# Layer 1's MLP by seven block products, its hidden layer through DRAM

## The chip, the core and the metric

One core of a Trainium2 chip runs the whole program. Its engines are TensorE (PE in the profile; PEld is its weight load), VectorE (DVE), ScalarE (ACT), GpSimd (POOL) and SyncE (SP, which issues the DMAs here). The metric is the device time of one execution in microseconds (us). All data is fp32.

## The reference

Two transformer layers over 1024 latent tokens and 256 context tokens, width 1024. Both layers have a mixer (attention) and a squared-ReLU MLP of width 4096, each between RMS norms with shift, scale and gate. After layer 1 only the latent tokens are kept, so its MLP works on 1024 tokens:

```python
def squared_relu_mlp(h, w1, w2):
    return jnp.square(jax.nn.relu(h @ w1)) @ w2

f_x = squared_relu_mlp(modulate(rms_norm(x, norm_g[l, 2]), sh2_x, sc2_x), w_mlp_in[l], w_mlp_out[l])
x = x + g2_x * rms_norm(f_x, norm_g[l, 3])
```

Here h is 1024 x 1024, w1 1024 x 4096 and w2 4096 x 1024: two matrix products of the same size.

## The kernel before, in words

The stages follow one another: layer 0 with its attention and its MLP, layer 1's input projection, its attention, its output projection and, from some 2551 us of the profiled execution, its MLP. The change is in the last two.

**A product.** Every fp32 operand of a projection or of the MLP is split into a high part (fp32r, the rounded form that TensorE takes) and a low part, the rest. `split` copies the high part on one engine and subtracts it from the source on another. `dense` adds three matmuls per 128 rows of the contraction: high by high, high by low, low by high. Each multiplies a stationary 128x128 block with a moving 128x512 one into a PSUM bank of 512 columns.

**Slots.** `R` hands out tiles of 128x1024 (4 KB a partition) by hand, with a life that says how long their memory stays. 12 of them live throughout; each span of the kernel adds its own. A slot is overwritten only once its last reader is done.

**The output projection** works tile by tile (128 tokens). A tile's two products go through `residual` (ACT squares, POOL's power, DVE's scaling, a sum on POOL or DVE) and then, one tile later, through `norm_T`: a norm, 8 transposes on TensorE, and `norm_half`, which applies scale and shift (ACT for the first half of the width, DVE for the second) and splits the result h into slots of `X` (`MlpIn`), in two chunks of 512 tokens.

**The MLP** (`mlp`) goes through 16 blocks of 256 hidden columns. A block's up products are two chunks of tokens by two 128-column halves, 24 matmuls each; ACT applies the ReLU, DVE squares and makes the high part, POOL the low part, and the result stays in slots. Its down products are 8 tiles by two halves of the width, 6 matmuls each; DVE adds each onto `acc`, a tile of 128x1024 per token tile, also in SBUF (the first block is copied by ACT). W1's and W2's blocks come through `stg`, a pool of two 128x1024 staging buffers, and are split by ACT and POOL during the block before. In the last block the tiles are finished in turn: a norm, the gate and the residual (`finish1`), then the store to the output. Inputs of the residual are loaded two tiles ahead, from three buffers.

**Order.** Tile's scheduler orders each engine's instructions from a timeline of its own; only where `manual_schedule` stands (attention, the last block of an MLP) is an engine's order as written. On the chip each engine's queue is worked off in that fixed order.

## Time and profile before

| what | value |
|---|---|
| median of three runs | 3286.07 us (3283.56 to 3288.95) |
| profiled execution | 3286.25 us, span 3284.4 us |
| TensorE busy | 3196.6 us, 97% of the span |
| DVE, ACT, POOL busy | 1547.1, 1117.9, 1056.1 us |
| mean granted clock of TensorE | 0.991 of full speed |
| layer 1's MLP | about 2551 to 3264 us of the span |

The span runs from the first to the last instruction; the execution's own time is 1.9 us longer. Busy time of TensorE counts each matmul from its start to its modelled end. Matmuls overlap, so how many of them fit into a stretch is read from their starts, not from their durations. A row of the timeline ends, in brackets, with the idle time before it and with what ended it.

### The profile page before, as it was taken

How to read it: one execution, taken by the hardware profiler on the slowest of the kernel's cores; microseconds unless marked ns; L12 is line 12 of the kernel's file. 1: busy time of each engine (PE TensorE's matmuls, PEld its weight loads, DVE VectorE, ACT ScalarE, POOL GpSimd, SP SyncE). 2: the span in 40 equal slices, each digit the busy share in tenths (PEclk: the TensorE clock that was granted, in tenths of full speed). 3: DMA queues.
4: the chain of work that ended last, by engine and by line, in shares of the span. 5: the costliest groups of instructions: out<-in, count | busy, mean ns of one | idle time of the engine just before them, and what ended most of it. 6: DMA issues, size and time to landing. Idle time of an engine off the chain costs nothing.

```text
span 3284.4 us, 47529 instructions
## 1 busy us (share of the span) xinstructions
PE 3196.6 (97%) x18421; PEld 2611.4 (80%) x18421; DVE 1547.1 (47%) x3295; ACT 1117.9 (34%) x2315; POOL 1056.1 (32%) x878
## 2 busy tenths in 40 slices
PE   8999999999999999999999989999989999999997
PEld 3777888887887777777778878998878788888886
DVE  3345476798462343343343561148755333333335
ACT  4212576788342111111111242257864311111111
POOL 2346100035452232232232453210334533333333
PEclk9999999999999999999999999999999999999999
DMA  7566312132432222222121146124454211111113
GB/s 242 166 150 177 81 53 57 55 85 87 138 116 84 71 63 84 64 71 85 57 65 39 58 145 153 44 60 118 130 152 127 73 45 52 52 45 51 46 46 96
DMA packets 221569, 294.00 MB, mean 90 GB/s; under 512 B 36800, under 2 KB 154064, under 8 KB 221344
## 3 DMA queue, kind: packets, MB, share of 16 engines
q1 hardware_dynamic: 221248, 290.71, 30.0%
q8 instruction: 145, 2.38, 0.3%
q14 instruction: 80, 0.66, 0.1%
q0 software_dynamic: 96, 0.26, 0.0%
HBM read 240.01 MB, written 50.89 MB: 89 GB/s over the span
## 4 chain that ended last, share of the span: by engine, by line
PE 75%; DVE 3%; issue 2%; DMA 2%; POOL 1%; ACT 1%; SPq 0%; POOLq 0%; ACTq 0%; DVEq 0%
PE mm L382 20%; PE mm L383 19%; PE mm L384 19%; PE po L1081 2%; PE tp L1060 2%; PE po L913 2%; PE md L246 1%; PE S L515 1%; PE X L516 1%; PE X L515 1%; PE S L516 1%; PE po L808 1%; PE tp L892 1%; PE tp L790 1%; POOL s L193 1%
## 5 line engine op out<-in xcount | busy, mean ns | idle before, releaser
L1198 DVE TENSOR_TENSOR acc<-mm,acc 128x512 f32<-128x512 f32 x540 | 369.1, 689 | 388.1 <-PE mm L384 387.1
L193 POOL TENSOR_TENSOR r<-ws,r 128x1024 fp32r<-128x1024 f32 x146 | 356.9, 2449 | 539.5 <-ACT r L186 534.8
L384 PE MATMUL mm<-s,r 128*128 128x512 f32 (+1 forms) x1404 | 516.6, 368 | 0.0
L383 PE MATMUL mm<-s,r 128*128 128x512 f32 (+1 forms) x1404 | 515.5, 367 | 0.0
L382 PE MATMUL mm<-s,r 128*128 128x512 f32 (+1 forms) x1404 | 513.5, 366 | 1.7 <-DVE s L188 1.7
L1184 DVE TENSOR_TENSOR hr<-hr 128x512 f32<-128x512 f32 (+1 forms) x160 | 134.4, 840 | 612.7 <-ACT hr L1183 612.6
L382 PE MATMUL mm<-r,r 128*128 128x512 f32 x1046 | 413.5, 395 | 0.3 <-DVE r L188 0.3
L383 PE MATMUL mm<-r,r 128*128 128x512 f32 x1046 | 408.5, 391 | 0.0
L384 PE MATMUL mm<-r,r 128*128 128x512 f32 x1046 | 407.9, 390 | 0.0
L186 ACT ACTIVATE r<-ws 128x1024 fp32r<-128x1024 f32 x155 | 164.4, 1061 | 709.2 <-PE mm L384 336.8
L193 POOL TENSOR_TENSOR r<-hr,r 128x512 fp32r<-128x512 f32 (+1 forms) x130 | 167.0, 1285 | 562.6 <-DVE r L188 559.2
L1183 ACT ACTIVATE hr<-mm 128x512 f32<-128x512 f32 (+1 forms) x160 | 88.3, 552 | 644.4 <-PE mm L384 638.4
L382 PEld LDWEIGHTS mm<-s,r 128*128 128x128 f32 x1404 | 264.2, 188 | 50.6 <-DVE s L188 1.9
L383 PEld LDWEIGHTS mm<-s,r 128*128 128x128 f32 x1404 | 264.7, 189 | 49.2
L384 PEld LDWEIGHTS mm<-s,r 128*128 128x128 f32 x1404 | 264.1, 188 | 46.1
L382 PEld LDWEIGHTS mm<-r,r 128*128 128x128 f32 x1046 | 196.2, 188 | 80.7 <-DVE acc L1198 36.9
L384 PEld LDWEIGHTS mm<-r,r 128*128 128x128 f32 x1046 | 196.3, 188 | 43.0 <-POOL r L193 0.9
L383 PEld LDWEIGHTS mm<-r,r 128*128 128x128 f32 x1046 | 196.4, 188 | 39.1
L713 ACT ACTIVATE P<-P,nm 128x1280 f32<-128x1280 f32 (+1 forms) x160 | 190.2, 1190 | 31.1 <-DVE P L721 28.7
L382 PE MATMUL mm<-r,e 128*128 128x512 f32 (+1 forms) x496 | 192.6, 389 | 1.3 <-ACT e L186 1.3
L383 PE MATMUL mm<-r,e 128*128 128x512 f32 (+1 forms) x496 | 190.9, 385 | 0.0
L384 PE MATMUL mm<-r,e 128*128 128x512 f32 (+1 forms) x496 | 189.8, 385 | 0.4 <-POOL e L193 0.4
(256 smaller groups left out, 6011.3 us busy)
## 6 DMA issues: line engine op xcount, KB each, us to landing
wm<-in_w_mod_dram SPq DMA_DIRECT2D x80, 512.0 KB
ws<-in_w_mlp_in_dram SPq DMA_DIRECT2D x64, 512.0 KB
ws<-in_w_mlp_out_dram SPq DMA_DIRECT2D x64, 512.0 KB
q<-qT SPq DMA_DIRECT2D x224, 128.0 KB
ws<-in_w_in_dram SPq DMA_DIRECT2D x36, 512.0 KB
xres<-xn SPq DMA_DIRECT2D x18, 512.0 KB
x<-xres SPq DMA_DIRECT2D x18, 512.0 KB
wm<-in_w_mod_dram SPq DMA_DIRECT2D x32, 256.0 KB
```

The source lines that it names most:

```text
L186: act.activation(o, i, AF.Copy)
L193: lo_eng.tensor_tensor(lo, src, f(hi), op=OP.subtract)
L382: pe.matmul(pt, sh, mh, start=k == 0, stop=False)
L383: pe.matmul(pt, sh, ml, start=False, stop=False)
L384: pe.matmul(pt, sl, mh, start=False, stop=k == n - 1)
L515: pe.matmul(dst, q[0], k, start=True, stop=False)
L516: pe.matmul(dst, q[1], k, start=False, stop=True)
L713: act.activation(P, P, AF.Exp, scale=-1.0, bias=self.nm[:, u:u + 1], accum_out=self.sums[:, u:u + 1])
L913: pe.matmul(self.po, VB[self.h][:, kt, :], self.pt[:, kt, :], start=kt == self.kts[0], stop=kt == self.kts[-1])
L1183: act.activation(r, pt, AF.Relu)
L1184: dve.tensor_tensor(r, r, r, op=OP.mult)
L1198: dve.tensor_tensor(acc[t][:, s], pt, acc[t][:, s], op=OP.add)
```

## The change

Both of the MLP's matrix products are cut into 2x2 blocks, and the four result blocks are formed from seven block products instead of eight (Strassen's method, in Winograd's form). `SEVEN` names, for either side, which operand block or which sum of blocks enters product 1 to 7; `TURN` is their order. Three PSUM banks take the products of a turn: 1, 6, 7 and 4 add up in bank b, product 2 is in a, 5 and 3 add up in c, and what b or c holds after each product is taken out before the next one adds to it.

**Up** (`up7`). The blocks of h are two halves of the width by two halves of the tokens (`Tokens7`: four raw tiles of 128x4x512). `norm_half` now writes h raw; only products 1 and 2, which take blocks 11 and 21 as they are, are split tile by tile. The other five operands come from `rest`, which forms its sums in place and splits them, called in front of the fifth product. W1 goes in 16 units of 256 columns. POOL forms the sums (4 of 7 products), ACT the high part and DVE the low part; a product's operand is one slot, and products are prepared six ahead. A product has 12 matmuls. ACT and DVE combine the results, and the squared ReLU goes to `hT`, a new tensor in DRAM, 4096 x 1024.

**Down** (`Down7`). The hidden layer comes back from `hT`, for 256 tokens and the rows of a unit. There are six units of 3, 3, 3, 3, 2 and 2 pairs of 128 hidden rows (m, with g as the index), four passes over pairs of token tiles in each (j), seven products in each pass; a product has 3m matmuls. The token side is stationary: DVE forms sums (4 of 7) and low parts, ACT the high parts, six products ahead. The weight side moves: for each g and product one slot, its sums and low part by POOL, its high part by ACT. Of the 28 slots, 21 hold unit 0 and 7 one g of unit 1. In the last pass of a unit, `weights` prepares m further operands after each product, in the slots that it freed. DVE adds each product's bank onto `acc` (in unit 0, ACT copies four of seven). After product 4 of a pass in the last unit, both of its tiles are finished.

The slots of h come free in the last up unit, product by product, and the down half's first operands go there. `bg`, a bias buffer of earlier stages, moves to a pool of its own, which is closed before layer 1's attention. The residual's input has one buffer now, and it is loaded when a tile is finished.

```diff
+UNITS1 = (3, 3, 3, 3, 2, 2)
...
+    def dense(pt, sta, mov, first=True, group=True):
+        n, free = len(sta), not group
         for k in range(n):
             (sh, sl), (mh, ml) = sta[k], mov[k]
-            pe.matmul(pt, sh, mh, start=k == 0, stop=False)
-            pe.matmul(pt, sh, ml, start=False, stop=False)
-            pe.matmul(pt, sl, mh, start=False, stop=k == n - 1)
+            pe.matmul(pt, sh, mh, start=first and k == 0, stop=False, skip_group_check=free)
+            pe.matmul(pt, sh, ml, start=False, stop=False, skip_group_check=free)
+            pe.matmul(pt, sl, mh, start=False, stop=k == n - 1, skip_group_check=free)
...
+    SEVEN = {"S": {1: (11,), 2: (12,), 4: (22,), 5: (21, OP.add, 22), 6: (5, OP.subtract, 11),
+                   7: (11, OP.subtract, 21), 3: (12, OP.subtract, 6)},
+             "T": {1: (11,), 2: (21,), 3: (22,), 5: (12, OP.subtract, 11), 6: (22, OP.subtract, 5),
+                   7: (22, OP.subtract, 12), 4: (21, OP.subtract, 6)}}
+    TURN = (1, 2, 6, 5, 7, 3, 4)
...
+        def get(self, p):
+            if p not in self.q:
+                r = self.rule[p]
+                if len(r) == 1:
+                    self.q[p] = self.q[r[0]]
+                else:
+                    a, b = self.get(r[0]), self.get(r[2])
+                    o = self.temp()
+                    self.add.tensor_tensor(o, a, b, op=r[1])
+                    self.q[p] = o
+            return self.q[p]
...
+        def rest(self, p, lo_eng=dve):
+            q = self.q
+            for c in range(2):
+                k = slice(2 * c, 2 * c + 2)
+                b11, b12, b21, b22 = (q[x][:, k, :] for x in (11, 12, 21, 22))
+                a, b = self.slots(p)[c]
+                if p == 5:
+                    dve.tensor_tensor(b11, b12, b11, op=OP.subtract)
+                elif p == 7:
+                    dve.tensor_tensor(b12, b22, b12, op=OP.subtract)
+                elif p == 6:
+                    dve.tensor_tensor(b22, b22, b11, op=OP.subtract)
+                elif p == 4:
+                    dve.tensor_tensor(b21, b21, b22, op=OP.subtract)
+                split(a, b, {5: b11, 7: b12, 3: b22, 6: b22, 4: b21}[p], act, lo_eng)
...
+            s = R.get(0)
+            v = s.view([128, 2, 4, 128])
+            split(v[:, 0], v[:, 1], W[u].get(p), act, dve)
+            ops[u, p] = s, [(v[:, 0, k, :], v[:, 1, k, :]) for k in range(4)]
...
+        for i, (u, p) in enumerate(seq):
+            if i < 14 and p not in (1, 2) and u == 0:
+                if p == 6:
+                    for x in (5, 7, 3, 6):
+                        X.rest(x)
+                elif p == 5:
+                    X.rest(4)
+            ready(len(seq) if u == n - 1 else i + ahead)
+            k = {1: "b", 2: "a", 5: "c"}.get(p)
+            if k:
+                st[u, k] = ps.tile([128, 512], F32, name=k, tag=k, bufs=2)
+            b = st[u, {1: "b", 6: "b", 7: "b", 4: "b", 2: "a", 5: "c", 3: "c"}[p]]
+            s, sta = ops.pop((u, p))
+            dense(b, sta, X.parts(p), first=k is not None, group=False)
+            s.free()
+            if u == n - 1:
+                X.free(p)
+                freed(p)
...
+            def put(fh, th, other):
+                t = tmp.tile([128, 512], F32, tag="ht", name="ht", bufs=2)
+                r = tmp.tile([128, 512], F32, tag="hr", name="hr", bufs=2)
+                if other is None:
+                    act.activation(t, b, AF.Relu)
+                    dve.tensor_tensor(r, t, t, op=OP.mult)
+                else:
+                    dve.tensor_tensor(t, b, other, op=OP.add)
+                    dve.scalar_tensor_tensor(r, t, 0.0, t, op0=OP.max, op1=OP.mult)
+                sp.dma_start(hT[u * 256 + fh * 128:u * 256 + (fh + 1) * 128, th * 512:(th + 1) * 512], r)
...
+        def weights(self, n, tmp):
+            for _ in range(min(n, len(self.todo))):
+                ui, g, p = self.todo.pop(0)
+                f0, m = self.units[ui]
+                if (ui, g) not in self.raw:
+                    r = []
+                    for x in (f0 + g, f0 + m + g):
+                        w = stg.tile([128, 1024], F32, tag="stg", name="ws", bufs=NSTG)
+                        sp.dma_start(w, w_mlp_out[self.l, x * 128:(x + 1) * 128, :])
+                        r.append(w)
+                    self.raw[ui, g] = Seven("T", {10 * (f + 1) + h + 1: r[f][:, h * 512:(h + 1) * 512]
+                                                  for f in range(2) for h in range(2)},
+                                            lambda: tmp().tile([128, 512], F32, tag="cm", name="cm", bufs=3), pool)
+                s = R.get(1)
+                v = s.view([128, 2, 512])
+                split(v[:, 0], v[:, 1], self.raw[ui, g].get(p), act, pool)
+                self.W[ui, g, p] = s, (v[:, 0], v[:, 1])
...
+                if (ui, j) not in H:
+                    raw = tmp.tile([128, 2 * mx, 256], F32, tag="hw", name="hw", bufs=2)[:, :2 * m]
+                    sp.dma_start(raw, self.hT[f0 * 128:(f0 + 2 * m) * 128, j * 256:(j + 1) * 256]
+                                 .rearrange("(a p) t -> p a t", p=128))
+                    H[ui, j] = Seven("S", {10 * (t + 1) + fh + 1: raw[:, fh * m:(fh + 1) * m, t * 128:(t + 1) * 128]
+                                           for t in range(2) for fh in range(2)},
+                                     lambda: tmp.tile([128, mx, 128], F32, tag="ch", name="ch", bufs=3)[:, :m], dve)
+                v = tmp.tile([128, 2, mx, 128], F32R, tag="ho", name="ho", bufs=ahead + 1)
+                split(v[:, 0, :m], v[:, 1, :m], H[ui, j].get(p), act, dve)
+                ops[ui, j, p] = [(v[:, 0, k, :], v[:, 1, k, :]) for k in range(m)]
...
+                k = {1: "b", 2: "a", 5: "c"}.get(p)
+                if k:
+                    st[k] = ps.tile([128, 512], F32, name=k, tag=k, bufs=2)
+                b = st[{1: "b", 6: "b", 7: "b", 4: "b", 2: "a", 5: "c", 3: "c"}[p]]
+                dense(b, ops.pop((ui, j, p)), [self.W[ui, g, p][1] for g in range(m)], first=k is not None, group=False)
+                if j == self.npairs - 1:
+                    for g in range(m):
+                        self.W.pop((ui, g, p))[0].free()
+                    self.weights(m, lambda: tmp)
+                t, h = {1: (0, 0), 2: (0, 0), 6: (0, 1), 3: (0, 1), 7: (1, 1), 5: (1, 1), 4: (1, 0)}[p]
+                o = acc[2 * j + t][:, h * 512:(h + 1) * 512]
+                if ui == 0 and p in (1, 6, 5, 4):
+                    act.activation(o, b, AF.Copy)
+                else:
+                    dve.tensor_tensor(o, b, o, op=OP.add)
+                if last and p == 4:
+                    for x in (2 * j, 2 * j + 1):
+                        finish(x, acc[x])
...
-    span = ExitStack()
-    R.add(span.enter_context(tc.tile_pool(name="span1", bufs=1, reuse_waits="tile")), 20, "s1", 1)
-    mid = span.enter_context(tc.tile_pool(name="mid1", bufs=1, reuse_waits="tile"))
-    ps = span.enter_context(tc.tile_pool(name="ps4", bufs=1, space=PSUM, reuse_waits="tile"))
-    X3 = MlpIn(T)
+    span, xs, sup = ExitStack(), ExitStack(), ExitStack()
+    R.add(span.enter_context(tc.tile_pool(name="span1", bufs=1, reuse_waits="tile")), 16, "s1", 1)
+    wp = ExitStack()
+    R.add(wp.enter_context(tc.tile_pool(name="wp0", bufs=1, reuse_waits="tile")), 4, "w0")
+    ps = sup.enter_context(tc.tile_pool(name="ps4", bufs=1, space=PSUM, reuse_waits="tile"))
+    X3 = Tokens7(xs.enter_context(tc.tile_pool(name="xraw", bufs=1, side="right", reuse_waits="tile")))
...
+    D1 = Down7(1, UNITS1, 4, hT, None)
+    ph = ExitStack()
+    R.add(ph.enter_context(tc.tile_pool(name="wp1", bufs=1, reuse_waits="tile")), 3, "w1")
+    tmp = ph.enter_context(tc.tile_pool(name="t5", bufs=1, reuse_waits="tile"))
+    ps = ph.enter_context(tc.tile_pool(name="ps5", bufs=1, space=PSUM, reuse_waits="tile"))
+    n7 = [0]
+    def freed(p):
+        n7[0] += 1
+        D1.weights((4, 4, 4, 4, 4, 1, 0)[n7[0] - 1], lambda: tmp)
+    for _ in up7(1, X3, ps, tmp, hT, 6, 4, freed):
+        pass
+    ph.close()
+    R.drop(7)
+    wp.close()
+    xs.close()
...
     def finish1(j, acc):
-        if j + XA < 8:
-            load1(j + XA)
-        residual([acc], G2[0], xts[j], acc, ps, pool if FIN1[j % len(FIN1)] == "P" else dve)
+        xt = tmp.tile([128, 1024], F32, tag="x", name="x", bufs=1)
+        sp.dma_start(xt, xres[2][j * 128:(j + 1) * 128, :])
+        residual([acc], G2[0], xt, acc, ps, pool if FIN1[j % len(FIN1)] == "P" else dve)
         sp.dma_start(block(out[0], j), acc)
 
-    with tc.tile_pool(name="t5", bufs=1, reuse_waits="tile") as tmp:
-        mlp(1, X3, 8, ps, mid, tmp, W1, finish1, last1,
-            [("up", 0), ("up", 1, 0), ("down", 0), ("down", 1), ("up", 1, 1), ("free", 0), ("free", 1), ("w1", 0)]
-            + [("down", i) for i in range(2, 8)])
+    D1.weights(7, lambda: tmp)
+    D1.run(acc, ps, tmp, 6, finish1, last1)
+    ph.close()
```

## Rows read from the trace of the kernel before

**Rows 1.** The page: busy us of each engine, share of the span, instructions.

```profile
PE 3196.6 (97%) x18421; PEld 2611.4 (80%) x18421; DVE 1547.1 (47%) x3295; ACT 1117.9 (34%) x2315; POOL 1056.1 (32%) x878
```

**Rows 2.** Busy time by stretch: stretch, us, engines (instructions), TensorE clock, DMA share, GB/s.

```profile
2563.00:2568.00 5.00, 1.78 (x12) 1.22 (x11) 3.80 (x11) 2.10 (x5) 2.64 (x4) 1.00 0.00 0
...
2700.00:3200.00 500.00, 500.00 (x2172) 407.48 (x2171) 183.05 (x269) 75.57 (x93) 167.95 (x92) 1.00 0.15 47
...
3200.00:3265.00 65.00, 64.17 (x280) 52.18 (x278) 36.54 (x52) 14.11 (x33) 26.90 (x18) 1.00 0.25 70
```

**Rows 3.** Timeline of TensorE: start, us; 15 starts in a row, then 51.

```profile
2699.70 0.39 PE L382 MATMUL mm<-s,r 128*128 128x512 f32 x1
...
2702.96 0.40 PE L384 MATMUL mm<-s,r 128*128 128x512 f32 x1
...
3252.45 0.39 PE L382 MATMUL mm<-r,r 128*128 128x512 f32 x1
...
3263.78 0.39 PE L384 MATMUL mm<-r,r 128*128 128x512 f32 x1
```

**Rows 4.** Groups of instructions, 2551 us on: count | busy us, mean ns | idle before.

```profile
L382 PE MATMUL mm<-s,r 128*128 128x512 f32 x512 | 201.1, 393 | 1.7 <-DVE s L188 1.7
...
L1198 DVE TENSOR_TENSOR acc<-mm,acc 128x512 f32<-128x512 f32 x240 | 165.3, 689 | 187.1 <-PE mm L384 186.5
...
L193 POOL TENSOR_TENSOR r<-hr,r 128x512 fp32r<-128x512 f32 x64 | 82.4, 1287 | 232.4 <-DVE r L188 232.0 <-DVE n1m L180 0.4
...
L1128 POOL TENSOR_TENSOR acc<-acc,x 128x1024 f32<-128x1024 f32 x6 | 15.7, 2612 | 8.0 <-DVE acc L1127 4.6 <-DVE nrm L180 1.9 <-ACT hr L1183 1.5
```

**Rows 5.** The same groups over the whole span: DVE by shape.

```profile
L193 DVE TENSOR_TENSOR s<-ws,s 128x1024 fp32r<-128x1024 f32 x4 | 5.0, 1290 | 12.0 <-ACT s L186 12.0
...
L1690 DVE TENSOR_TENSOR q<-tp,q 128x256 fp32r<-128x256 f32 x32 | 13.4, 418 | 2.4 <-ACT q L186 2.3
```

**Rows 6.** Timeline of DVE and of POOL at three places.

```profile
2713.79 1.91 DVE L1184 TENSOR_TENSOR hr<-hr 128x512 f32<-128x512 f32 x1
...
2712.75 2.40 POOL L193 TENSOR_TENSOR r<-ws,r 128x1024 fp32r<-128x1024 f32 x1 [0.40 <-ACT r L186]
...
2724.08 0.69 DVE L1198 TENSOR_TENSOR acc<-mm,acc 128x512 f32<-128x512 f32 x1 [0.67 <-PE mm L384]
...
2723.23 2.40 POOL L193 TENSOR_TENSOR r<-ws,r 128x1024 fp32r<-128x1024 f32 x1 [5.22 <-ACT r L186]
...
3247.21 1.28 DVE L1127 SCALAR_TENSOR_TENSOR acc<-acc,nrr,gate 128x1024 f32<-128x1024 f32 x1 [2.96 <-POOL nrr L181]
...
3248.54 0.69 DVE L1184 TENSOR_TENSOR hr<-hr 128x512 f32<-128x512 f32 x1
...
3248.64 2.85 POOL L1128 TENSOR_TENSOR acc<-acc,x 128x1024 f32<-128x1024 f32 x1 [1.46 <-ACT hr L1183]
```

**Rows 7.** Timeline at the start of the MLP: TensorE, ACT, DVE.

```profile
2564.84 1.09 PE L308 MATMUL tr<-ident,xt 128*128 128x128 f32 x8 [1.56 <-DVE xt L301]
...
2567.60 0.73 PE L382 MATMUL mm<-s,r 128*128 128x512 f32 x2 [1.66 <-DVE s L188]
...
2552.97 1.06 ACT L186 ACTIVATE r<-ws 128x1024 fp32r<-128x1024 f32 x1 [1.62 <-DMA ws<-in_w_mlp_out_dram]
...
2553.94 0.58 ACT L178 ACTIVATE xn<-mm 128x512 f32<-128x512 f32 x1
...
2558.82 1.22 DVE L1128 TENSOR_TENSOR xn<-xn,xt 128x1024 f32<-128x1024 f32 x1
...
2565.98 1.37 DVE L315 TENSOR_SCALAR h<-tr,mcols 128x128 f32<-128x128 f32 x4
```

**Rows 8.** Chain of waits (start, us, what); SP's waits, 2500:2600 (total, times, longest).

```profile
2549.43 3.52 DMA ws<-in_w_mlp_out_dram
...
SPq L353 <- POOL r L193: 37.1, 5, 23.1
```

**Rows 9.** Chain of waits at the end of the span.

```profile
3266.56 9.05 DMA x<-xres
```

More of the change, by code (lines that the diff above doesn't have):

```diff
@@ L394, in hybrid_dit_kernel @@
     os0 = dscr([NT * 128, 1024], "os0")
+    hT = dscr([FF, T], "hT")
     def block(a, j):
@@ L1296, in out_projection, with __init__ @@
         return out
+    SEVEN = {"S": {1: (11,), 2: (12,), 4: (22,), 5: (21, OP.add, 22), 6: (5, OP.subtract, 11),
[3 more added lines that the diff above has]
+    TURN = (1, 2, 6, 5, 7, 3, 4)
+    class Seven:
+        def __init__(self, side, blocks, temp, add):
+            self.rule, self.q, self.temp, self.add = SEVEN[side], dict(blocks), temp, add
+        def get(self, p):
[9 more added lines that the diff above has]
+            return self.q[p]
@@ new lines, in hybrid_dit_kernel, with __init__, slots, tile @@
+    class Tokens7:
+        def __init__(self, pool):
+            self.q = {10 * (kh + 1) + th + 1: pool.tile([128, 4, 512], F32, name=f"xq{kh}{th}")
+                      for kh in range(2) for th in range(2)}
+            self.s = {}
+        def slots(self, p):
+            if p not in self.s:
+                self.s[p] = [(R.get(1), R.get(1)) for _ in range(2)]
+            return [tuple(x.view([128, 2, 512]) for x in ab) for ab in self.s[p]]
+        def tile(self, i):
+            th, o = divmod(i, 4)
+            o = slice(o * 128, (o + 1) * 128)
+            def parts(h):
+                if th:
+                    return []
+                return [(2 * c, 2, a[:, :, o], b[:, :, o]) for c, (a, b) in enumerate(self.slots(1 + h))]
+            parts.raw = lambda h: self.q[10 * (h + 1) + th + 1][:, :, o]
+            return parts
+        def rest(self, p, lo_eng=dve):
[13 more added lines that the diff above has]
+                split(a, b, {5: b11, 7: b12, 3: b22, 6: b22, 4: b21}[p], act, lo_eng)
+        def parts(self, p):
+            return [(a[:, k, :], b[:, k, :]) for a, b in self.slots(p) for k in range(2)]
+        def free(self, p):
+            for ab in self.s.pop(p):
+                for x in ab:
+                    x.free()
@@ L1754, in last1 @@
+    ph.close()
+    R.drop(7)
+    wp.close()
+    xs.close()
+    ph = ExitStack()
+    tmp = ph.enter_context(tc.tile_pool(name="t6", bufs=1, reuse_waits="tile"))
+    ps = ph.enter_context(tc.tile_pool(name="ps6", bufs=1, space=PSUM, reuse_waits="tile"))
+    acc = [tmp.tile([128, 1024], F32, name=f"acc{t}") for t in range(8)]
+    G2 = {}
     def last1():
-        gate_next(1, 0)
-        for j in range(XA):
-            load1(j)
+        G2[0] = stg.tile([128, 1024], F32, tag="stg", name="gate", bufs=NSTG)
+        mod_vec(G2[0], 1, 5, 0)
```

97 lines of the change are left out of this document (81 added, 16 removed).

## The prediction

> **What bounds the kernel now.** I read the page's busy shares first, then a table by stretches of layer 1's MLP, then matmul starts in the timeline, then the other engines beside them. TensorE is busy 97% of the span [rows 1], and in the MLP (2551 to 3264 us) its only gap is near 2565, of 3.2 us in two waits; in 2700 to 3200 us DVE is busy 183 of 500 us, ACT 76, POOL 168 [rows 2]. So this stretch is bound by the number of matmuls and by nothing else. A matmul's 390 ns is latency: starts lie (2702.96 - 2699.70)/14 = 0.2329 us apart in an up product and (3263.78 - 3252.45)/50 = 0.2266 us in a down product [rows 3]. Three groups of 512 are of the first kind, three of the second, and one of the six stands in [rows 4]; so the MLP is 1536 x 0.2329 + 1536 x 0.2266 = 705.8 us of TensorE.
>
> **What the change removes.** Seven products for eight: 2688 matmuls for 3072, so 313.0 + 304.6 us for 357.7 + 348.1, which is **-88.2 us**. The two rates may go with where the operands lie; all matmuls at one or the other rate would give -79.8 or -96.7. Before 2551 us I expect no change: the output projection only loses a split on DVE and POOL in its last four tiles.
>
> A product is now short. Up: 12 matmuls, 2.79 us. Down: 9 matmuls (units of m=3) or 6 (m=2), 2.04 or 1.36 us; 28 products a unit, 57.1 or 38.1 us. What must keep up per product is priced from rows: a 128x512 evacuation on DVE from PSUM 0.69, POOL's 128x512 op 1.29 [rows 4]; a DVE op of 256 columns 0.42, of 1024 columns from SBUF 1.22 to 1.29, and so 0.55 for 384 [rows 5, 7]; ACT's op of 512 columns 0.58, taken as 0.6 [rows 7].
>
> **What is new: POOL's weights for the down half.** For each of 16 row pairs g of W2 POOL makes 7 subtractions for the low halves and 4 sums: 11 x 1.29 = 14.2 us, 227 us in all, where before it was busy 168 of 500 us and nothing waited for it. The place is what matters: 28 slots hold one unit (21) and one further g (7). A unit's slots come free only in its last pass (j=3), product by product, and the next unit's first pass needs two more g's, 22 POOL ops. Nor do raw rows run ahead: they share two staging buffers, so each new g waits some 2.5 us of its load's 3.5 us [rows 8].
>
> **A lock between POOL and DVE.** A DVE op with both inputs in SBUF that starts while POOL runs ends only 0.55 us after POOL's end: 1.91 us for a 0.69 us op at 2713.79, under POOL's 2712.75 to 2715.15. An evacuation from PSUM at 2724.08 under the same kind of POOL op takes its 0.69. POOL waits too: 2.85 us for 2.40 at 3248.64, behind DVE's 3248.54 [rows 6]. The Trainium skill has this as a rule (SBUF — State Buffer, Who interferes with whom): a DVE instruction with two SBUF inputs and a GpSimd one that reads SBUF exclude each other for the whole instruction, and the second blocks; the trace agrees by those numbers. By that rule terms (d) and the lock's part of (b) and (c) below stand; without it they would fall away and the sum would end near the first rival's.
>
> In the down half DVE issues 11 such ops per 7 products (7 low halves, 4 sums), 1.57 per product. Where POOL always has work, DVE and POOL alternate: 1.29 + 0.55 less 0.14 at either change of hands = 1.56 us a pair, so 1.57 x 1.56 = 2.45 us a product against TensorE's 2.04; for m=2 it is 1.57 x 1.43 = 2.24 against 1.36. Evacuations fit beside POOL's op.
>
> **(a) Into the up half: +15 us** (10 to 20). Four products run while the last tokens are normalized; the fifth needs X.rest of 5, 7, 3 and 6: 6 subtractions and 8 low halves of 128x1024, 14 x 1.22 = 17.1 us on DVE, after the last tile's h. That h ended at 2567.35; its tile's first square started only at 2553.94, behind copies of W2 rows that leave ACT here, so I take 2565. Product five then starts at 2582. Of 2551.2 to 2582, 11.2 are products and 1.1 transposes: 18.5 us idle against 1.56 + 1.66 before [rows 7].
>
> **(b) Into the down half: +24 us** (17 to 30). X's slots come free product by product in the last up unit (19.6 us), the raw rows land about 14 us before its end. Unit 0 needs 33 POOL ops: 42.6 us + two raw gaps 5 + DVE's share 3 - 14 = 36.6 us after the up half's end, + the last product 2.0 = 38.6 for a pass of 14.3.
>
> **(c) Units 0 to 1, 1 to 2, 2 to 3: +33 us** (3 x 6.5 to 3 x 16). From the first slot (2.0 us into j=3): 22 POOL ops 28.4 + a raw gap 2.5 + an ACT copy 0.6 = 31.5, + the last product 2.0: two passes take 35.5 instead of 28.6, +7 with no lock. With 22 DVE ops in between at 0.3 us each it is +13.5. A part of DVE's ops falls into POOL's own waits for ACT; I take +11. From unit 3 to 4 only one g is missing, 11 ops, which are in time.
>
> **(d) The lock where nothing else waits: +20 us** (5 to 30). Pass j=1 of units 0 to 3 runs beside 11 POOL ops: 7 x 0.41 = 2.9 each, taken 2.5, +10. Unit 3's last pass +2. Unit 4 runs beside 22: 14 products x 0.88 = 12, taken 8.
>
> **(e) The end: +7 us** (3 to 14). Unit 5 finishes two tiles a pass: two scalings of 1.28 us on DVE [rows 6] and POOL adds of 2.6 [rows 4], against 9.5 us of matmuls with 18 DVE ops of 9.4 us: +4. At the very end two tiles remain, and with one x buffer for three the second's load waits for the first's sum; before, the last load took 9.05 us [rows 9]: +3.
>
> **(f) The rest: +2 us** (0 to 8). The up half is covered: per 19.6 us DVE has 14 ops of 0.69 and POOL four of 1.29; ACT 11 copies of 0.6; the hT stores and loads, some 32 MB over 600 us, add little to a DMA share of 0.15 [rows 2]. W2's loads move onto SP into the last passes, each waiting there for a staging buffer that POOL frees (a load for POOL has waited 23.1 us on SP, [rows 8]), and the hT loads queue behind them; these run one pass ahead, 9.5 to 14.3 us, and the rest would be up to 8. Products on one PSUM bank have another between them, 2.0 us for an evacuation of 0.69. No row of before shows a chain of waits on one bank.
>
> **Sum.** -88.2 + 15 + 24 + 33 + 20 + 7 + 2 = +12.8 us. The profiled execution took 3286.25 us (span 3284.4), 0.2 above the median of three: 3286.25 + 12.8 = **3299 us**, 0.4% slower. TensorE's share falls, and POOL's chain sets the ends of four passes.
>
> **Rivals.** *First, faster: the waits coincide.* POOL waits for ACT's high half (0.60) and for raw rows anyway; if DVE's ops fall into just these, the lock costs next to nothing: (a) 12, (b) 19, (c) 21, (d) 5, (e) 4, (f) 0 = 61, so -27, **3259 us**. For it: outside a unit's first pass DVE has slack, and six products are prepared ahead. Against it: alternation is what the rows show wherever both have work. It decides once all losses stay under 82 us; the 7 us per transition of (c) and 17 of (b) stand even then. Chance 0.25. *Second, the gain in full*: preparation hidden everywhere and (a) alone left, 3286 - 88 + 15 = **3213 us**; the 28 slots speak against it. 0.03. *Third, much slower: the order on the queues.* DVE and ACT take their work in a fixed order. Where a weight's high half waits on ACT for raw rows that wait for POOL, the operands of the next products queue behind it, and every DVE op pays POOL's full op: 20 + 30 + 48 + 30 + 14 + 8 = 150, so +62, **3348 us**. For it: at 2552.97 ACT has waited 1.62 us for W2 rows, with that square behind it [rows 7]. Against it: six products of lead. 0.18. *Fourth*, the terms balance within 0.2% (6.6 us, about what this kernel's measurement can tell from no change): 0.14.
>
> **Chances and range.** The forecast (3293 to 3330) has 0.40. Faster by over 0.2%: 0.25 + 0.03 = 0.28; same 0.14; slower 0.40 + 0.18 = 0.58. The bounds of the terms reach from 3252 (54.5 lost) to 3348 (150 lost); I leave a tenth on either side: 3256 to 3350.
>
> **What would show it.** Right: in the changed profile TensorE waits 15 to 20 us at the start of the up half and 20 to 30 us between the halves; in the down half its gaps lie in the first pass of units 0 to 3, and end with a POOL op that writes a weight slot; DVE ops with two SBUF inputs last 1.0 us and more while POOL works, evacuations 0.69; the up half runs at 2.79 us a product. Wrong: gaps between products spread over the up half, or ended by a DMA of hT or by an evacuation; POOL idle at the start of unit 1; DVE's sums at 0.55 us beside a busy POOL; matmul starts further apart than 0.233 us with all operands there.

## The result, and the profile after

Runs of both kernels on one chip: 3286.18 us before and **3333.85 us** after (3330.52 to 3341.27), a ratio of 1.0148, interval [1.0129, 1.0167]. The change makes the kernel 1.5% slower. The forecast was 3299 us, 0.4% slower, with a range of 3256 to 3350: the side and the range held, but the loss is 48 us and not 13.

The page of the changed kernel (busy us, share of the span of 3332.7 us, instructions), beside [rows 1]:

```profile
PE 3135.0 (94%) x18037; PEld 2549.6 (77%) x18037; DVE 1796.4 (54%) x3567; ACT 1262.1 (38%) x2653; POOL 1178.9 (35%) x976
```

384 matmuls are gone and TensorE is busy 62 us less, in a span that is 48 us longer. Where it stands still is seen by stretch (the columns of [rows 2]: stretch, us, PE, PEld, DVE, ACT, POOL, clock, DMA share, GB/s):

```profile
2560.00:2600.00 40.00, 30.97 (x111) 23.83 (x112) 36.28 (x38) 19.36 (x28) 20.67 (x8) 0.81 0.17 50
2700.00:2800.00 100.00, 100.00 (x436) 81.67 (x435) 57.40 (x71) 33.42 (x58) 33.17 (x22) 1.00 0.34 114
2880.00:2920.00 40.00, 5.31 (x23) 4.00 (x22) 5.66 (x7) 12.79 (x22) 39.12 (x31) 0.61 0.43 147
2980.00:3010.00 30.00, 26.52 (x107) 20.61 (x106) 25.26 (x27) 12.65 (x26) 25.09 (x18) 0.94 0.32 106
3280.00:3330.00 50.00, 0.00 (x0) 0.00 (x0) 7.24 (x8) 1.45 (x4) 6.81 (x6) 0.50 0.37 92
```

In 2700 to 2800 us the up half is bound by matmuls alone, as before: the cheaper products do pay there. Between the halves POOL works 39 of 40 us and TensorE 5. In the last 50 us no engine works for more than 8. Two starts of TensorE that waited, then POOL and DVE at the start of the up half:

```profile
2576.20 0.80 PE L390 MATMUL b<-s,w 128*128 128x512 f32 x1 [7.90 <-ACT w L191]
...
2919.70 0.80 PE L390 MATMUL b<-s,ho 128*128 128x512 f32 x1 [34.69 <-ACT ho L191]
```

```profile
2559.56 1.27 POOL L1331 TENSOR_TENSOR cm<-ws 128x512 f32<-128x512 f32 x1 [2.89 <-PE tr L317]
2560.91 9.64 POOL L1331 TENSOR_TENSOR cm<-cm,ws 128x512 f32<-128x512 f32 x1
2570.52 1.27 POOL L1331 TENSOR_TENSOR cm<-ws 128x512 f32<-128x512 f32 x1
...
2560.80 2.35 DVE L1367 TENSOR_TENSOR xq<-xq,xq 128x1024 f32<-128x1024 f32 x2
...
2571.25 1.08 DVE L198 TENSOR_TENSOR w<-cm,w 128x512 fp32r<-128x512 f32 x1 [1.81 <-ACT w L191]
```

The same POOL op takes 1.27 us and 9.64 us. In the long one DVE ran its row of two-input ops over h from 2560.80 to 2569.44 us, one after the other, and POOL got no turn: its op ended at 2570.55, in DVE's first pause.

Within the down half TensorE's waits have another end than the forecast gave them. From 2930 to 3229 us the longest in total, then one of them on TensorE and what DVE did before it:

```profile
PE b L390 <- DVE acc L1537: 19.6, 12, 5.4
...
2995.21 0.79 PE L390 MATMUL b<-r,ho 128*128 128x512 f32 x1 [2.94 <-DVE acc L1537]
...
2993.04 1.51 DVE L1331 TENSOR_TENSOR ch<-ch,hw 128x384 f32<-128x384 f32 x1
2994.47 0.68 DVE L1537 TENSOR_TENSOR acc<-b,acc 128x512 f32<-128x512 f32 x1
```

A product waits for its bank, until DVE has added the product before onto `acc`. That addition takes its usual 0.68 us, but it stands in DVE's queue behind token operations of up to 1.64 us for 0.55. No wait of units 0 to 4 ends with a POOL operation on a weight slot.

The chain of waits at the end (start, us, what), where [rows 9] had one load:

```profile
3257.18 8.51 DMA x<-xres
...
3265.82 2.38 POOL acc L1137
...
3269.19 8.90 DMA x<-xres
...
3278.23 2.33 POOL acc L1137
...
3315.41 8.65 DMA x<-xres
...
3324.16 1.23 DVE acc L1137
```

The last matmul starts at 3276.27 us. What follows is a row of loads of the residual's input through one buffer: load 8.5 to 8.9, add 2.4, store issued 0.6, next load; from 3269.19 to 3281.33 (the next two loads' starts) that is 12.1 us a tile. On SP a load also stands behind the store of the tile before it, which waits for the same sum:

```profile
3280.59 0.63 SPq L2025 DMA_DIRECT2D out_dram<-acc  x1
3281.33 0.39 SPq L2023 DMA_DIRECT2D x<-xres  x1
```

So the one buffer and the place of the load on SP both hold it back; no run has only one of them.

**The account.** Passes are counted from matmul starts, 63 or 42 matmuls each in TensorE's order (which mixes the products of neighbouring passes, so that a pass here is a count), ideal passes at the rates of [rows 3] (14.3 us for m=3, 9.5 for m=2). What is over in the changed kernel, less what the kernel before lost in the same place:

| term | forecast | measured |
|---|---|---|
| seven products for eight | -88.2 | -88.2 (assumed; the rest closes on it) |
| (a) into the up half | +15 | +15.0 (22.2 beyond the matmuls' own time, 7.2 before) |
| (b) into the down half | +24 | +43.8 (34.9 without a matmul, then a first pass of 23.2) |
| (c) units 0 to 1, 1 to 2, 2 to 3 | +33 | +10.4 (passes of 15.6 + 19.2, 16.2 + 15.7, 14.6 + 14.9) |
| (d) lock elsewhere | +20 | +23.4 (second passes of 16.8 to 18.6; unit 4 11.7 in all) |
| (e) the end | +7 | +45.1 (unit 5 9.3; 56.4 from the last matmul's start, 20.7 before) |
| (f) and the MLP's earlier start | +2 | -1.4 |
| sum | +12.8 | +48.1 (spans: 3332.7 - 3284.4 = 48.3) |

These terms contain a cost that no forecast names: TensorE's clock. The MLP of the kernel before and of this one, by stretch:

```profile
2551.00:3264.00 713.00, 709.78 (x3089) 578.10 (x3087) 268.42 (x399) 124.36 (x178) 253.23 (x146) 1.00 0.17 51
...
2549.00:3277.00 728.00, 645.81 (x2708) 514.39 (x2706) 525.49 (x680) 270.88 (x520) 379.92 (x250) 0.95 0.30 98
```

Behind its long waits TensorE's matmuls start 0.43 us apart in place of 0.23 for a while (2578.08 and 2578.50 us, after the wait of 7.90): from 2577 to 2581 us the granted clock is 0.50, the lower of its two levels (1.2 of 2.4 GHz). 57 starts of the changed MLP are of this kind and none of the MLP before: an estimate of 11 us from these spacings, spread over (a) to (e).

### The profile page after: what moved, and what is told of

The parts are those of the page before. It is cut to its first block, busy times and chain, and to the rows that moved or that the text cites. A ratio compares the mean times of both kernels' runs of the same rounds, so it can differ in the third digit from the quotient of the medians.

```text
span 3332.7 us, 47986 instructions
## 1 busy us (share of the span) xinstructions
PE 3135.0 (94%) x18037; PEld 2549.6 (77%) x18037; DVE 1796.4 (54%) x3567; ACT 1262.1 (38%) x2653; POOL 1178.9 (35%) x976
## 5 line engine op out<-in xcount | busy, mean ns | idle before, releaser
L198 POOL TENSOR_TENSOR r<-ws,r 128x1024 fp32r<-128x1024 f32 (+1 forms) x102 | 236.1, 2321 | 320.3 <-ACT r L191 320.2
L391 PE MATMUL mm<-s,r 128*128 128x512 f32 (+1 forms) x892 | 313.5, 351 | 0.0
L392 PE MATMUL mm<-s,r 128*128 128x512 f32 (+1 forms) x892 | 312.4, 350 | 0.0
L390 PE MATMUL mm<-s,r 128*128 128x512 f32 (+1 forms) x892 | 312.2, 350 | 0.0
L1207 DVE TENSOR_TENSOR acc<-mm,acc 128x512 f32<-128x512 f32 x300 | 203.8, 688 | 197.5 <-PE mm L392 197.2
L191 ACT ACTIVATE r<-ws 128x1024 fp32r<-128x1024 f32 (+1 forms) x109 | 107.8, 991 | 414.0 <-DMA ws<-in_w_mlp_out_dram 284.1
L390 PE MATMUL mm<-r,r 128*128 128x512 f32 x534 | 214.0, 401 | 0.3 <-DVE r L193 0.3
L391 PE MATMUL mm<-r,r 128*128 128x512 f32 x534 | 209.0, 391 | 0.0
L392 PE MATMUL mm<-r,r 128*128 128x512 f32 x534 | 208.8, 391 | 0.0
L390 PEld LDWEIGHTS mm<-s,r 128*128 128x128 f32 x892 | 168.0, 188 | 25.8
L391 PEld LDWEIGHTS mm<-s,r 128*128 128x128 f32 x892 | 168.5, 189 | 24.5
L392 PEld LDWEIGHTS mm<-s,r 128*128 128x128 f32 x892 | 168.0, 188 | 23.8
L1331 POOL TENSOR_TENSOR cm<-ws 128x512 f32<-128x512 f32 x64 | 97.0, 1516 | 192.1 <-DMA ws<-in_w_mlp_in_dram 174.5
L191 ACT ACTIVATE pt<-tp 128x512 f32<-128x512 f32 (+1 forms) x264 | 142.2, 552 | 51.8 <-PE tp L799 28.5
L390 PE MATMUL mm<-r,e 128*128 128x512 f32 (+1 forms) x400 | 153.4, 384 | 1.5 <-ACT e L191 1.2
L391 PE MATMUL mm<-r,e 128*128 128x512 f32 (+1 forms) x400 | 151.7, 379 | 0.0
L392 PE MATMUL mm<-r,e 128*128 128x512 f32 (+1 forms) x400 | 151.0, 379 | 0.2 <-POOL e L198 0.2
L390 PEld LDWEIGHTS mm<-r,r 128*128 128x128 f32 x534 | 100.2, 188 | 60.3 <-DVE acc L1207 36.9
```

Of the source, the lines that this page charges most:

```text
L191: act.activation(o, i, AF.Copy)
L198: lo_eng.tensor_tensor(lo, src, f(hi), op=OP.subtract)
L390: pe.matmul(pt, sh, mh, start=first and k == 0, stop=False, skip_group_check=free)
L391: pe.matmul(pt, sh, ml, start=False, stop=False, skip_group_check=free)
L392: pe.matmul(pt, sl, mh, start=False, stop=k == n - 1, skip_group_check=free)
L1207: dve.tensor_tensor(acc[t][:, s], pt, acc[t][:, s], op=OP.add)
```

## The experiments

The theory at this point: the end is the one x buffer's row of loads; the slow passes are the lock of DVE and POOL; the gap between the halves is POOL's row of weights. All ratios are against the kernel before on the same chip; differences in us between versions cross chips, on which the kernel before took 3285.3 to 3287.9 us. One difference goes with no edit: in nine of the versions' profiles the up half lasts 328.1 to 329.6 us and not 324.4, so differences under 5 us between profiles decide nothing. In seven of these nine a second POOL op at its start is held for 4.9 to 5.3 us under DVE's row; in the changed kernel none is.

**1. t_x: the end.** The inputs of the last sums are fetched four tiles ahead, into weight slots that are free by then.

```diff
-        xt = tmp.tile([128, 1024], F32, tag="x", name="x", bufs=1)
-        sp.dma_start(xt, xres[2][j * 128:(j + 1) * 128, :])
+        xs7[j] = R.get(1)          # for j+4, when j is done; 0 to 3 in last1
+        sp.dma_start(f(xs7[j].view([128, 1024])), xres[2][j * 128:(j + 1) * 128, :])
```

> The changed kernel with one edit: in the last unit the residual's inputs are loaded into four free weight slots ahead of need (tiles 0 to 3 at the unit's start, then one per finished tile), instead of one buffer that a tile's load gets only when the tile before it is summed. Theory (the tail is a chain of eight loads of 8.5 us and sums of 2.4 us through one buffer): the time from the last matmul to the end falls from 56.4 us to 18 to 24, the last unit's last pass from 18.0 to 10 to 11.5 us, the whole by 38 to 46 us, to 3288 to 3296 us. Rival (two tiles finishing at once are bound by ACT, POOL and DVE, whatever the load does): the tail stays over 35 us and the whole falls by less than 20.

3303.9 us, ratio 1.0054 [1.0039, 1.0069]; 17.7 us behind the last matmul, from 56.4. The loads were the end: 30 us of the 48, where 38 to 46 were expected. The edit gives more buffers and an earlier place on SP at once, so it does not tell which of the two held the loads. The last pass still took 18.4 us; there too the expectation missed. DVE and POOL in that pass:

```profile
3261.16 2.29 DVE L198 TENSOR_TENSOR ho<-ch,ho 128x256 fp32r<-128x256 f32 x1
...
3267.27 2.48 DVE L198 TENSOR_TENSOR ho<-ch,ho 128x256 fp32r<-128x256 f32 x1
...
3270.28 0.41 DVE L198 TENSOR_TENSOR ho<-hw,ho 128x256 fp32r<-128x256 f32 x1
```

```profile
3260.76 2.39 POOL L1137 TENSOR_TENSOR acc<-acc,s 128x1024 f32<-128x1024 f32 x1 [3.38 <-ACT md L183]
...
3267.14 2.33 POOL L1137 TENSOR_TENSOR acc<-acc,s 128x1024 f32<-128x1024 f32 x1
```

A DVE op of 0.41 us takes 2.3 to 2.5 when it starts under POOL's residual add: it ends 0.3 us behind it, much as in [rows 6].

**2. no_lock: the slow passes.** The second input of all eleven token operations comes from a PSUM bank of zeros, so the sums and low halves are not the reference's.

```diff
-                split(v[:, 0, :m], v[:, 1, :m], H[ui, j].get(p), act, dve)
+                src = H[ui, j].get(p)
+                act.activation(v[:, 0, :m], src, AF.Copy)
+                dve.tensor_tensor(v[:, 1, :m], src, z3[:, :m], op=OP.subtract)
```

> The changed kernel, its down half's DVE ops on the token side (7 low halves and 4 sums per seven products) with the second input from a bank of PSUM that holds zeros, in place of one in SBUF: as many ops of the same size, but each with one SBUF input; the sums and low halves are then not those of the reference. Theory (a DVE op with two SBUF inputs and a POOL op exclude each other): these ops fall from a mean of 0.90 to 1.26 us to about 0.55 for 384 columns, POOL's from 1.56 to 1.27; the second pass of units 1 to 3 falls from 16.8, 17.8, 18.6 to 14.5 us, unit 4's first two passes from 11.7 and 18.6 to 9.7, the first pass of units 0 and 1 by 5 us each; the whole falls by 20 to 32 us. Rival (DVE and POOL are slow because of their own queues and waits, not through a lock): the durations stay and the whole moves by less than 5 us.

3302.13 us, ratio 1.0052 [1.0035, 1.0069]. Groups from 2930 to 3200 us (count, busy us, mean ns, idle before), the changed kernel and then this one:

```profile
L198 DVE TENSOR_TENSOR ho<-ch,ho 128x384 fp32r<-128x384 f32 x61 | 53.5, 876 | 11.4 <-ACT ho L191 11.2
L198 POOL TENSOR_TENSOR s<-cm,s 128x512 fp32r<-128x512 f32 x31 | 48.4, 1569 | 0.0
...
L1331 DVE TENSOR_TENSOR ch<-ch,hw 128x384 f32<-128x384 f32 x15 | 18.6, 1240 | 0.5
```

```profile
L198 POOL TENSOR_TENSOR s<-cm,s 128x512 fp32r<-128x512 f32 x31 | 39.9, 1299 | 0.9 <-ACT s L191 0.9
L1521 DVE TENSOR_TENSOR ho<-ch,z 128x384 fp32r<-128x384 f32 x60 | 32.8, 548 | 15.0 <-PE b L392 11.9 <-PE a L392 1.9 <-PE c L392 0.8
```

DVE's op falls from 876 or 1240 ns to 548, POOL's from 1569 to 1299 (the forecast's pair was 1.56 us), and from the second pass of unit 0 to unit 4 every pass is ideal to 0.3 us. The edit is worth 32 us. Not all of this need be the lock: the low half no longer reads ACT's high half, so DVE's wait for it (11.2 us in the first row) goes as well, and some 4 us are the lower clock behind waits that are gone (an estimate as above). The next run, ch_psum, keeps DVE's wait for ACT. The gap between the halves (34.3 us for 34.7) and the end (56.1) stay.

**3. ch_psum: part of it.** The sums 5, 6 and 3 go to PSUM, so five of the eleven operations are free of the lock. The squares of the last norms share their two banks.

```diff
-                                     lambda: tmp.tile([128, mx, 128], F32, tag="ch", name="ch", bufs=3)[:, :m], dve)
+                                     lambda x: ps.tile([128, 512], F32, tag="md", name="md", bufs=2)... if x != 7 else
+                                     tmp.tile([128, mx, 128], F32, tag="ch", name="ch", bufs=3)[:, :m], dve)
```

> The sums of products 5, 6 and 3 on the token side of the down half go to two PSUM banks in place of SBUF, so that five of the eleven VectorE operations of a pass (the sums 6 and 3, the low halves 5, 6 and 3) read one input from PSUM; six still read two inputs from SBUF. The result is the reference's. Theory (the shared lock of VectorE and GpSimd costs some 32 us in the down half, as the kernel with all eleven freed showed): these five take 0.55 us in place of 0.91 to 1.26, and 5/11 of the 32 us go: -14 us, 3320 (3314 to 3326). Rival (the lock only costs where all of VectorE's operations are slow together, since what is left still falls behind GpSimd's row): under 6 us, 3328 to 3334.

3307.71 us, ratio 1.0061 [1.0046, 1.0077], 26 us gained and not the 14 of a fair share. Units 0 to 4 take 278.4 us, for 309.4 in the changed kernel and 273.2 with all eleven freed: the six that are left cost 5 of the 36 us and not 20. TensorE's waits for DVE's additions, 19.6 us above, are 1.2 here. That fits a threshold better than a sum: at 1.56 us a pair, eleven pairs in seven products are 2.45 us a product against TensorE's 2.04, and six are 1.34. But this counts neither the other five operations nor the additions, and no run has another number of locked operations, so the threshold is argued and not shown. Unit 5 and the end together stay (103.3 us for 103.6): the row of loads hides what its products do.

**4. h_first, lo_dve0 and h_own: the gap between the halves.** h_first issues the second unit's first seven weights behind the first token loads; lo_dve0 makes unit 0's 21 low halves on DVE; h_own gives the first two token loads memory of their own and issues them in the last up unit. This is the program's order; where nothing else is fixed, Tile's scheduler makes its own.

```diff
+                if i == 0:                          # h_first, in run(); the call ahead of run() goes
+                    self.weights(7, lambda: tmp)
...
-                split(v[:, 0], v[:, 1], self.raw[ui, g].get(p), act, pool)
+                split(v[:, 0], v[:, 1], self.raw[ui, g].get(p), act, lo)       # lo_dve0: dve for unit 0
...
+        if n7[0] == 1:                              # h_own, in freed()
+            xs.close()
+            D1.hp = hs.enter_context(tc.tile_pool(name="hp", bufs=1, side="right", reuse_waits="tile"))
+            D1.pre = {j: D1.load(0, j) for j in range(2)}
```

> The changed kernel with one edit: the first seven weight operands of unit 1 are prepared after the first loads of the hidden layer from DRAM in program order, not before them. Theory (TensorE waits 34.7 us between the halves because SP holds the hidden layer's load behind W2 loads that wait for POOL): unit 0's own operands are complete some 7 us before the load is issued now, so the wait falls by 6 to 10 us and the whole by 4 to 10. Rival (unit 0's 33 POOL ops set the start, the load is late only because nothing needs it earlier): the first matmul comes earlier but the first pass ends where it ends now, and the whole moves by less than 2 us.

> The changed kernel with one edit: the 21 low halves of unit 0's weights are formed by DVE, which has nothing to do in 28 us of the gap between the halves, and not by POOL; POOL keeps their 12 sums. Theory (the gap of 34.7 us and the slow first pass are unit 0's chain of 33 POOL ops): that chain falls from 33 x 1.27 to some 12 x 1.3 + 21 x 0.7 us, partly at the same time, so the gap falls by 10 to 20 us and the whole by 10 to 22. Rival (the load of the hidden layer behind W2's loads sets the gap, through the two staging buffers and 3.5 us a load): these loads come no closer than their own 3.8 us each, eight of them some 30 us, and the whole falls by less than 6 us.

> As the changed kernel, but the down half's first two token loads have memory of their own (that of h's raw blocks, long read by then) and are issued in the last up unit, ahead of the weight loads for the down half. Theory (the first pass ran behind GpSimd's row of weights and not beside it, since the token load came at its end): the first product starts well under 34 us after the up half's end, the first pass waits for weights in its middle instead, and its end comes 10 to 20 us earlier: 3333.9 - 15 = 3319 (3313 to 3325). Rival (GpSimd's row sets the end of the first pass by itself, and VectorE's token operations beside it stretch it by the lock, 33 x 0.27 = 9 us): the first product is early, the pass is longer by as much, under 5 us gained: 3329 to 3337.

h_first: 3338.48 us, 1.0161 [1.0146, 1.0176], the gap unchanged (35.1 us). But it did not test its theory, for SP's order did not change. SP in h_first:

```profile
2908.81 3.99 SPq L1486 DMA_DIRECT2D ws<-in_w_mlp_out_dram  x2
2916.14 0.96 SPq L1505 DMA_DIRECT2D hw<-hT  x2
```

These two weight loads are the seventh and eighth; unit 0 needs six, and in the changed kernel too eight stand ahead of the tokens (the last two from 2907.92 us, the tokens at 2912.03). lo_dve0: 3325.38 us, 1.0118 [1.0098, 1.0138], 8.5 us gained, between the two theories; the gap is 22.4 us. So POOL's row is in the gap. What ends the gap there is the token load, again behind eight weight loads:

```profile
2910.26 0.94 ACT L191 ACTIVATE ho<-hw 128x384 fp32r<-128x384 f32 x2 [1.42 <-DMA hw<-hT]
```

h_own: 3335.71 us, 1.0152 [1.0138, 1.0165], no gain; its theory fell. SP issued its token loads at 2656.6 us already. Gap and first pass are 52.5 us for 58.1, but the up half was 4.5 us longer in this execution. What holds the first product is read on ACT and DVE, in the changed kernel and then in h_own:

```profile
2911.38 0.63 ACT L191 ACTIVATE r<-ws 128x512 fp32r<-128x512 f32 x1 [2.82 <-DMA ws<-in_w_mlp_out_dram]
...
2915.38 1.15 ACT L191 ACTIVATE r<-ws 128x512 fp32r<-128x512 f32 x2 [2.85 <-DMA ws<-in_w_mlp_out_dram]
2918.60 0.63 ACT L191 ACTIVATE r<-cm 128x512 fp32r<-128x512 f32 x1 [2.07 <-POOL cm L1331]
2919.14 0.92 ACT L191 ACTIVATE ho<-hw 128x384 fp32r<-128x384 f32 x2
...
2917.61 1.37 DVE L1331 TENSOR_TENSOR ch<-hw 128x384 f32<-128x384 f32 x1 [28.01 <-DMA hw<-hT]
```

```profile
2923.20 1.15 ACT L191 ACTIVATE r<-ws 128x512 fp32r<-128x512 f32 x2 [2.61 <-DMA ws<-in_w_mlp_out_dram]
2924.25 0.92 ACT L191 ACTIVATE ho<-hw 128x384 fp32r<-128x384 f32 x2
...
2924.79 0.80 DVE L198 TENSOR_TENSOR ho<-hw,ho 128x384 fp32r<-128x384 f32 x1 [25.79 <-ACT ho L191]
```

In h_own the tokens are there, and the first `ho` waits for nothing but its turn: ACT takes its work in order, high halves of weights stand ahead of it, and each of them waits for a sum of POOL's or for raw rows that wait for POOL's staging buffer. The last ones are not even needed yet: their rows are the seventh and eighth weight loads (in h_own from 2916.03 us), which are unit 1's. In the changed kernel the load is late as well, so taking away one of the two waits left the other. A version in which unit 1's weights stand behind the first tokens on SP and ACT, as h_first meant it, was not measured.

**5. w1_dve: the start of the up half.** The weight sums of the first two units go to DVE.

```diff
-                             .rearrange("p (a n) -> p a n", a=4), pool)
+                             .rearrange("p (a n) -> p a n", a=4), dve if u < 2 else pool)
```

> The eight weight sums of the up half's first two units are made by VectorE in place of GpSimd. Theory (GpSimd is starved at the start of the up half by VectorE's row of two-input operations, and the second unit's weights come 7.9 us late for it): the wait of 7.9 us is gone or under 3 us, -4 to -8 us: 3326 to 3330. Rival (VectorE, in order, was the late one all along, and eight more operations of about 0.55 us make it later): 3334 to 3339, and the waits move to products 5 and 4 of the first unit.

3336.94 us, 1.0148 [1.013, 1.0166]: no gain. TensorE's waits for the first weights fall to 3.2 us from 7.9, and the up half lasts 322.7 us for 324.4, so DVE did starve POOL there, and the long POOL op is gone. The rival's time held, though not its reason: the gap behind the up half grew by 3.5 us, and why is open: POOL waited 16.6 us for raw rows before and in it, for 12.3.

**6. units_x: the row shortened.** On t_x, with units of 2, 3, 3, 3, 3 and 2 pairs, so that the first unit needs 22 POOL operations and not 33.

```diff
-UNITS1 = (3, 3, 3, 3, 2, 2)
+UNITS1 = (2, 3, 3, 3, 3, 2)
```

> As the kernel with the inputs of the last sums fetched into free weight slots (3303.9), and the down half's units are of 2, 3, 3, 3, 3 and 2 row blocks in place of 3, 3, 3, 3, 2 and 2, with the second unit's first fourteen weights made ahead. Theory (the gap between the halves and the slow first pass are GpSimd's row of 33 operations for the first unit): 22 are left, 11 x 1.29 us = 14 us less: 3290 (3286 to 3295); the gap falls from 34.7 us to some 25, the first pass is near its ideal of 9.5 us. Rival (the loads set it: two weight loads of 3.5 us fewer): -7 us, 3297. Second rival (the second unit's 21 weights are then late, since the first lasts 38 us and not 58): a new wait of 5 to 15 us at the start of the second unit, 3300 to 3310.

3292.08 us, 1.0014 [1.0006, 1.0023]: 11.8 us gained on t_x, near the 14 of the theory; the gap is 20 us. The first two passes were not ideal (17.4 and 18.5 us for 9.5), nor the second unit's first (22.2 for 14.3): part of what the shorter row gives is lost behind it. That the lock takes it is likely, for with sums in PSUM (best1, below) these passes take 14.4, 10.5 and 15.9, but lo_dve0's edit is in that version too.

**7. best1, best2, best3, best4: the edits together.** best1 has t_x, units_x, lo_dve0 and ch_psum; best2 also sends the squares of the last norms to SBUF; best3 adds w1_dve and h_first, best4 instead h_own.

```diff
-        residual(..., ("md", 2))          # best1: the squares share the two banks of the sums
+        residual(..., ("sq", 2, tmp))     # best2
```

> Four edits together: inputs of the last sums fetched early into weight slots, units of 2, 3, 3, 3, 3 and 2, the first unit's low halves on VectorE, and the token sums 5, 6 and 3 in PSUM. If the causes add: 3303.9 - 14 (units) - 5 (14 low halves on VectorE, where 21 gave 8.5 us) - 12 (five of eleven operations out of the lock) = 3273 (3265 to 3282), faster than the kernel before by some 0.4%. Rival (the gap is held by its loads once GpSimd's row is shorter, and the last pass by VectorE's finish): 3283 to 3292, no faster than before.

> As the kernel with four edits (3258.9), and the squares of the last norms go to SBUF in place of the PSUM banks that the token sums 6, 5 and 3 use. Theory (its last unit lost 18 us, 57.3 in place of 39, for the token sums waited for the squares' banks: ScalarE's `ho` waited 13.4 us for VectorE's sums, and these stood behind the scalings): without the shared banks the last unit takes 45 to 50 us: 3250 (3243 to 3254). Rival (VectorE is the bound there by itself: 7 sums of 0.6, 11 token operations of 0.42, two scalings of 1.2 and GpSimd's locks make over 11.7 us in a pass of 9.5): 3256 to 3261.

> As the kernel before this one, and the up half's first two units' weight sums on VectorE, and the second unit's first fourteen weights behind the down half's first token loads. Theory: the wait at the start of the up half falls from 10.7 us to about 5, and the gap between the halves from 15 us to about 10, since the token load no longer stands behind weight loads: -6 to -10 us more than the kernel before this one: 3242 (3236 to 3250). Rival (as in the two kernels with these edits alone, GpSimd's row and its loads begin at the last up unit and their end does not move): within 3 us of the kernel before this one.

> The same edit on the fastest kernel so far (3248.6; its first product waits 13.5 us for the token side). Theory: 5 to 10 us less, 3241 (3237 to 3245). Rival (the 22 operations of GpSimd's row and its weight loads set the first pass there already): 3246 to 3251.

best1 3258.9 us, 0.9917 [0.9903, 0.9931], 14 us below its expectation, which had put the sums in PSUM at 12 us. With the gains as measured alone the causes add: 3303.9 - 11.8 (units_x) - 26.1 (ch_psum) - 5.7 (two thirds of lo_dve0's 8.5) = 3260.3. Its last unit took 57.3 us, ScalarE waiting for sums whose banks the squares held:

```profile
ACT ho L191 <- DVE md L1331: 13.4, 4, 7.9
```

best2 3248.57 us, **0.9878 [0.9862, 0.9895]**, as expected: with the squares elsewhere this wait is 3.8 us and the last unit takes 47.4. It beats the kernel before by 1.2% and the changed one by 2.7% (0.9878 / 1.0148 = 0.973). best3 (3250.59, 0.9884 [0.987, 0.9899]) and best4 (3250.34, 0.9884 [0.9867, 0.9901]) are no faster, within their rivals' times. In best3, as in h_first, SP's order did not change: six weight loads stand ahead of the tokens in it and in best2, and its first unit needs four.

## Why the prediction was right, and where its size was off

**What held.** The change does not pay as it stands: -88.2 us of matmuls against waits that cost more, in the stages named. (a) measured 15.0 for 15, by luck: the forecast had four products run while the last tokens are normalized and then a wait for DVE's row over h. In fact TensorE waited 6.83 us for the last tile's norm before the first product, and then 7.90 for weights whose sums POOL could not make under that row. (d) measured 23.4 for 20, and the pair of 1.56 us is the row of 1569 ns; no_lock and ch_psum show that the lock makes these passes slow. That the total fell into the range owes something to (c): its 23 us too many cover part of the 58 that (b) and (e) had too few.

**The road of the lock was another.** The forecast had DVE's additions "fit beside POOL's op", its gaps "end with a POOL op that writes a weight slot", and gaps ended by an evacuation as a sign of being wrong. This sign came: from 2930 us to the end of unit 4, 19.6 us of TensorE's waits end with an addition that stood behind locked operations on DVE. The price of a pair was right, and the step from it to TensorE was not. Another such sign came too, matmul starts further apart than 0.233 us with all operands there: the lower clock, which the sum has at nothing.

**(e), +45.1 for +7, is the term that was mis-sized most.** The step reads "with one x buffer for three the second's load waits for the first's sum: +3". The mechanism was named, and counted for the last two tiles only. But seven of the eight loads wait for the tile before them: at some 12 us a tile the row needs 24 us a pass, against 9.5 us of matmuls, so it falls behind from the second tile on, and what is behind at the last matmul is paid in full. [rows 9] gave 9.05 us for a load; times seven it would have told. t_x removed it: 56.4 to 17.7 us.

**(b), +43.8 for +24.** The step put the end of POOL's row 36.6 us after the up half's end and only the last product behind it. The row came out shorter: its 33rd operation, counted from 2864.71 us and without one of unit 1's, ended at 2915.24, 30.2 us after the up half's end. What failed is the overlap: no product of the first pass ran beside the row, for ACT's first `ho` stood behind high halves of weights, the last of them unit 1's, and the token load behind eight weight loads. So the first product started after 34.9 us, and the pass of 23.2 came after it. This is the third rival's mechanism, the order on the queues, in one place. lo_dve0 and units_x show the row in it (8.5 and 11.8 us), h_own that the load alone is not the reason; what the order on SP and ACT is worth stays open.

**(c), +10.4 for +33.** The step has "+7 with no lock" at each transition, for a row of 22 POOL operations begun 2.0 us into the last pass, and a raw gap of 2.5. With no lock the transitions cost nothing. TensorE and POOL around the last pass of unit 0 in no_lock, which by count began at 2967.6 us:

```profile
2963.44 0.39 PE L390 MATMUL a<-s,ho 128*128 128x512 f32 x1
...
2963.88 2.56 POOL L198 TENSOR_TENSOR s<-ws,s 128x512 fp32r<-128x512 f32 x2 [26.98 <-ACT s L191]
...
2988.99 1.28 POOL L198 TENSOR_TENSOR s<-cm,s 128x512 fp32r<-128x512 f32 x1
2991.26 1.31 POOL L1331 TENSOR_TENSOR cm<-ws,cm 128x512 f32<-128x512 f32 x1 [0.99 <-DMA ws<-in_w_mlp_out_dram]
```

The row starts 3.7 us ahead of the pass as counted and has one gap of 1.0 us: 7 us better than the step had it, just its "+7". It can, because TensorE's order is the scheduler's: product 2 of this pass, the fourth to use bank a, starts at 2963.44 us, 6 us ahead of its place by count, so product 1 frees its slots that much earlier. What is left with the lock, 10.4 us, goes by DVE's additions as above. So (c) priced a chain that its cover hides, and (b) and (e) trusted a cover that was not there.

**Rivals.** Of the first (the waits coincide) nothing held but (c). The second's price (3213) was not reached by any version. The third named what (b) showed, and the additions on DVE's queue, but its other prices, (c) 48 and (e) 14, were not what made the time.

## What to carry to other kernels

Where work goes through one buffer, count the whole row (load, use, store, times the number of tiles) against the time that its cover lasts, and not the last link alone. Cover has to be shown on each queue that takes its work in order: a product can run beside a row of preparations only if its own operand does not stand behind them on ACT or SP, and it ends in time only if the addition that frees its bank does not stand behind slow work on DVE. An edit of the program's order is a test only if the trace shows that the queue's order changed. And a lock need not be taken away whole: the version that won kept the same products and took five of eleven operations out of it.

## What the runs showed of the hardware that was not expected

- Under DVE's unbroken row of operations with two SBUF inputs, a POOL operation of 1.27 us lasted 9.64: in this row the two did not alternate, and POOL ended in DVE's first pause. The op lasts 9.63 to 9.65 us in all eleven profiles that have it on POOL, and another beside DVE's later row 5.28 in t_x. The forecast's pair of 1.56 us is what the lock costs where both come by turns. That it is DVE's readiness that decides is inferred.
- A DVE operation with one input in PSUM keeps 0.55 us beside a busy POOL (no_lock, and 546 ns in ch_psum), and POOL's own operations fall from 1.57 to 1.30 us where all eleven are so; moving a temporary sum to PSUM is enough.
